# A decoder layer on one Trainium2 core: the filler stream of the first phase yields at every fourth channel tile instead of every second

## The chip, the core and the metric

The kernel runs on one core of a Trainium2 chip. A core has five engines that matter here, each with its own queue of instructions in fixed order: PE (TensorE, matmuls), DVE (VectorE), ACT (ScalarE), POOL (GpSimd) and SP (SyncE, which issues the DMAs). PE writes to PSUM, the others move results from there. The metric is the time of one execution on the device in microseconds.

## What is computed

One hybrid layer on a sequence of 2048 rows of 1024 channels: a norm, one input projection into 26 column tiles of 128, an RWKV-7 group (8 heads, a recurrence with a matrix state), a gated linear attention group (4 heads), an output projection with residual, a norm, a SwiGLU FFN with residual, and a last norm. Cut to what matters:

```python
n = rms_norm(h, rms1_g)
z = n @ w_in                                   # 26 tiles of 128 columns
y_rwkv = rwkv7_mixer(z[..., :D_RWKV_IN], ...)  # S = S*w + (S a) b + v k ; y = S r, step by step
y_gla = gla_mixer(z[..., D_RWKV_IN:], ...)     # in chunks of 64
h = h + concat([y_rwkv, y_gla]) @ w_out
n = rms_norm(h, rms2_g)
h = h + (silu(n @ ffn_gate) * (n @ ffn_up)) @ ffn_down
return rms_norm(h, final_g)
```

## The kernel before

The first phase takes the rows in four blocks of 512. For each block, 26 column tiles `zd` of the input projection are computed. A tile is 8 channel tiles (k = 0 to 7) with three matmuls each: weights and rows are split into a high and a low part, and high x high, high x low and low x high are summed in one PSUM tile (lines 630 to 632). A block so has 26 x 24 = 624 of these matmuls, the phase 2496. Two PSUM tiles, `zd0` and `zd1`, take turns.

All else in the phase are streams, written as Python generators that emit instructions and then `yield`. The list (line 433) has, among others:

- "b" (`stage_b`): the RWKV recurrence, 16 head pairs of 8 steps, four head pairs to a block. A step is `yp` on PE (L1333), `uv` on DVE (L1338), `ch` on PE (L1343), the new state `S` on DVE (L1349), and then `yp` of the next step. After the last step come a norm, the transposes `ytp` (L1380), `gp` (L1383), and the mark `b` with the number of the head pair.
- "a" and "a2": what the recurrence needs for each head pair (`u`, `ssp`, `rbp`, `vp`, `scp`, `bkp`, `bp`; and `atp`, `upp`, `zt`, `xt`, `wtp`, with a long chain `lt`, `lm` on POOL).
- "g" (`gmix`): the linear attention (`gkp`, `gds`, `gsc`, `gop`, `gotp`).
- "e" (`evac`): takes each `zd` tile out of PSUM, in the order of the tiles. It marks `ze` with the tile's number, for which the filler waits two tiles later. In `lora_g`, the evacuation of tile 11 (of tile 14 in the last block), it also waits for a head pair:

```python
        yield used
        if b:
            yield f"b{b * HP - 1}"
```

- "w" (weights: high part on ACT, L605, low part on POOL, L607), "x" and "p" (the normed rows of the next block, transposed by `tch`, L572).
- after the last `zd` tile, the out-projection `op` (32 jobs of 24 matmuls, L902 to L904), whose results are added to `hx`, and the preparation of the FFN's input ("np", "nt"): loads `hk`, transposes `tcn` (L1028), splits into `n` (L1058, L1060). It starts when the last head pair is marked.
- "z", the filler: `zmm`, which issues the `zd` matmuls, and then `out_mm` with those of `op`. It is the only stream marked as filler.

A planner (`Order.run`) puts all streams into one order, by its own estimates of when each engine is free. After each `yield` it picks the stream with the earliest time; the filler's time is at least that at which PE is free, less `AHEAD` (400 ns):

```python
            s = min(q, key=lambda s: (max(s[0], pe - self.AHEAD) if s[4] else s[0], s[1]))
```

So what the filler emits between two yields stands in PE's queue in one piece, and only then can another stream's matmuls follow. A stream that waits for a mark that is not yet set is out of the choice until it is. The FFN behind the phase (`up` with L1573 to L1575, `down`) is put in order by other means, and a few of its matmuls are moved ahead of the last `op`.

Of the kernel before, what the change touches and what calls it, by code (L numbers as in the profile page):

```python
# [269 lines left out]
class K:  # L270
# [341 lines left out]
    def zmm(self, nb):  # L612

        nc = self.nc
        self.zps = {}
        for b in range(nb):
            for i in range(NZ):
                yield f"w{b}.{i}"
                if i > 1:
                    yield f"ze{b}.{i - 2}"  # L620
                else:
                    yield f"prep{b}.{KT - 1 if i else KT // 2 - 2}"
                whi, wlo = self.wz.pop((b, i))
                ps = self.zd("zd", [128, BLK], i)
                for k in range(KT):
                    if not i and not k % 2:
                        yield f"prep{b}.{k}"
                        yield f"prep{b}.{k + 1}"
                    nh, nl = [t[:, k % 2] for t in self.nhl[b, k - k % 2]]
                    nc.tensor.matmul(out=ps, lhsT=whi[:, k, :], rhs=nh, start=(k == 0), stop=False)  # L630
                    nc.tensor.matmul(out=ps, lhsT=whi[:, k, :], rhs=nl, start=False, stop=False)  # L631
                    nc.tensor.matmul(out=ps, lhsT=wlo[:, k, :], rhs=nh, start=False, stop=(k == KT - 1))  # L632
                    if i == NZ - 1 and k % 2:
                        yield ("set", f"zk{b}.{k // 2}")
                    elif k % 2:
                        yield
                self.zps[b, i] = ps
                yield ("set", f"zm{b}.{i}")
# [1125 lines left out]
```

## Time and profile before

| | |
|---|---|
| median of 2 runs | 2765.57 us (2763.24 to 2767.9) |
| the profiled execution | 2761.73 us |
| its span | 2759.9 us, so 1.8 us lie around it |
| mean granted clock of PE | 0.978 |
| busy: PE, DVE, ACT, POOL | 95%, 56%, 44%, 45% of the span |

The span is that of the instructions in the trace. Busy time of PE counts pipelined matmuls as a union, so that a gap in it is a true gap. The granted clock is the share of full TensorE speed that the chip gave; idle time of an engine is put down to what it waited for last.

### The profile page before, as it was taken

Reading aid. Unit: us, or ns where it says so; the run is one execution under the profiler, and the core shown is the slowest. Engines: PE = TensorE matmul, PEld = TensorE weight load, DVE = VectorE, ACT = ScalarE, POOL = GpSimd, SP = SyncE. Lnnn points to the kernel's source line nnn. Section 1 sums busy time; section 2 is a strip of 40 time slices with the busy share of each in tenths; the row PEclk is TensorE's granted clock in tenths of the full one; section 3 lists DMA queues with packets and bytes.
Section 4 is the critical chain, followed back from the end, with each engine's and each line's share of the span. In section 5 each row is a group of like instructions: output and inputs, shape, how many; then the busy total and the mean of one; then the engine's idle time right before and its main releaser. Section 6 shows DMA issues by size and latency. Waiting matters only on the chain.

```text
span 2759.9 us, 40039 instructions
## 1 busy us (share of the span) xinstructions
PE 2616.7 (95%) x14328; PEld 2102.5 (76%) x14328; DVE 1534.0 (56%) x2950; ACT 1219.0 (44%) x2363; POOL 1244.8 (45%) x1866
## 2 busy tenths in 40 slices
PE   6899899989998999999899999999999999999998
PEld 4777677867786777777678787888777888888886
DVE  5456756676666566756655445453647444443354
ACT  7455644665455555544543333342433333332232
POOL 3656555646564476510466566500007555550000
PEclk9999999999998999999999999999999999999999
DMA  4212311232122212456523333265633222224462
GB/s 146 63 58 77 92 55 47 81 100 62 50 69 62 62 59 65 150 176 206 168 92 116 121 118 127 88 214 145 223 127 121 83 84 77 85 85 136 142 225 91
DMA packets 175847, 300.02 MB, mean 109 GB/s; under 512 B 15776, under 2 KB 65664, under 8 KB 175648
## 3 DMA queue, kind: packets, MB, share of 16 engines
q1 hardware_dynamic: 175648, 297.46, 33.8%
q8 instruction: 113, 1.85, 0.3%
q14 instruction: 86, 0.70, 0.1%
HBM read 241.83 MB, written 55.57 MB: 108 GB/s over the span
## 4 chain that ended last, share of the span: by engine, by line
PE 71%; DVE 10%; POOL 6%; DMA 4%; ACT 4%; issue 3%; SPq 1%; DVEq 0%; POOLq 0%; ACTq 0%
PE up L1575 10%; PE up L1574 10%; PE up L1573 10%; PE dn L1648 6%; PE dn L1647 5%; PE dn L1646 5%; PE zd L630 4%; PE zd L632 4%; PE zd L631 4%; DMA hx<-in_x 2%; POOL lm L1249 2%; POOL w_lo L607 2%; POOL lt L1247 2%; PE ch L1343 1%; PE scp L1172 1%
## 5 line engine op out<-in xcount | busy, mean ns | idle before, releaser
L607 POOL TENSOR_TENSOR w_lo<-w_raw,w_hi 128x512 fp32r<-128x512 f32 x208 | 278.9, 1344 | 239.3 <-ACT w_hi L605 203.9
L1070 POOL TENSOR_TENSOR ws<-S,ws 128x512 fp32r<-128x512 f32 x176 | 248.8, 1416 | 289.7 <-ACT ws L1068 280.3
L1579 DVE TENSOR_TENSOR C<-up,C 128x512 f32<-128x512 f32 x308 | 208.4, 689 | 286.5 <-PE up L1575 286.2
L630 PE MATMUL zd<-nh,w_hi 128*128 128x512 f32 x832 | 356.8, 429 | 6.3 <-DVE k L673 3.3
L632 PE MATMUL zd<-nh,w_lo 128*128 128x512 f32 x832 | 333.6, 401 | 8.4 <-POOL w_lo L607 8.4
L631 PE MATMUL zd<-nl,w_hi 128*128 128x512 f32 x832 | 331.1, 398 | 1.5 <-DVE nl L577 1.5
L1574 PE MATMUL up<-n,ws 128*128 128x512 f32 x704 | 278.2, 395 | 4.5 <-DVE n L1060 4.4
L1573 PE MATMUL up<-n,ws 128*128 128x512 f32 x704 | 278.1, 395 | 2.8 <-ACT n L1058 2.8
L1648 PE MATMUL dn<-wd,hh 128*128 128x512 f32 x704 | 279.3, 397 | 0.1
L1575 PE MATMUL up<-n,ws 128*128 128x512 f32 x704 | 278.3, 396 | 0.0
L1647 PE MATMUL dn<-wd,hh 128*128 128x512 f32 x704 | 277.9, 395 | 0.0
L1646 PE MATMUL dn<-wd,hh 128*128 128x512 f32 x704 | 277.4, 394 | 0.0
L1068 ACT CAST ws<-S 128x512 fp32r<-128x512 f32 x176 | 108.5, 620 | 306.7 <-PE up L1575 298.7
L1687 POOL TENSOR_TENSOR h<-h,hx 128x512 f32<-128x512 f32 x12 | 17.8, 1487 | 414.7 <-DMA hx<-hs 311.7
L1249 POOL TENSOR_TENSOR lm<-lm,lt 128x60 f32<-128x60 f32 (+24 forms) x496 | 180.2, 363 | 38.9
L632 PEld LDWEIGHTS zd<-nh,w_lo 128*128 128x128 f32 x832 | 159.4, 192 | 49.4 <-POOL w_lo L607 12.9
L1247 POOL TENSOR_TENSOR lt<-lm,ln 128x60 f32<-128x60 f32 (+24 forms) x496 | 154.3, 311 | 92.9 <-DVE ln L1231 69.3
L1639 DVE TENSOR_TENSOR hh<-hr,hh 128x512 fp32r<-128x512 f32 x88 | 66.2, 752 | 233.7 <-ACT hh L1637 232.9
L630 PEld LDWEIGHTS zd<-nh,w_hi 128*128 128x128 f32 x832 | 160.4, 193 | 38.1 <-issue 4.4
L631 PEld LDWEIGHTS zd<-nl,w_hi 128*128 128x128 f32 x832 | 160.6, 193 | 28.2 <-DVE nl L577 2.3
L1637 ACT CAST hh<-hr 128x512 fp32r<-128x512 f32 x88 | 54.5, 619 | 288.5 <-PE dn L1647 284.0
L1574 PEld LDWEIGHTS up<-n,ws 128*128 128x128 f32 x704 | 133.4, 189 | 36.9 <-DVE n L1060 5.8
(275 smaller groups left out, 5888.5 us busy)
## 6 DMA issues: line engine op xcount, KB each, us to landing
w_raw<-in_win SPq DMA_DIRECT2D x208, 256.0 KB, 2.6
raw<-in_wd SPq DMA_DIRECT2D x88, 512.0 KB, 3.6
raw<-in_wg SPq DMA_DIRECT2D x44, 512.0 KB, 3.5
raw<-in_wu SPq DMA_DIRECT2D x44, 512.0 KB, 3.6
hid<-C SPq DMA_DIRECT2D x88, 256.0 KB, 2.0
hr<-hid SPq DMA_DIRECT2D x88, 256.0 KB, 2.7
mraw<-mix SPq DMA_DIRECT2D x64, 256.0 KB, 4.0
xk<-in_x SPq DMA_DIRECT2D x32, 256.0 KB, 3.7
```

The lines of the kernel that those rows point to most:

```text
L607: nc.gpsimd.tensor_tensor(out=wlo[:, ks, :], in0=raw, in1=whi[:, ks, :].bitcast(F32), op=ALU.subtract)
L630: nc.tensor.matmul(out=ps, lhsT=whi[:, k, :], rhs=nh, start=(k == 0), stop=False)
L631: nc.tensor.matmul(out=ps, lhsT=whi[:, k, :], rhs=nl, start=False, stop=False)
L632: nc.tensor.matmul(out=ps, lhsT=wlo[:, k, :], rhs=nh, start=False, stop=(k == KT - 1))
L1070: eng.tensor_tensor(out=hl[:, 1], in0=src, in1=hl[:, 0].bitcast(F32), op=ALU.subtract)
L1249: nc.gpsimd.tensor_tensor(out=lm[:, 0:j, i0:], in0=lm[:, 0:j, i0:], in1=lt[:, 0:j, i0:], op=ALU.add)
L1573: nc.tensor.matmul(out=ps, lhsT=w[:, 0, ks], rhs=h, start=(k == 0), stop=False)
L1574: nc.tensor.matmul(out=ps, lhsT=w[:, 0, ks], rhs=l, start=False, stop=False)
L1575: nc.tensor.matmul(out=ps, lhsT=w[:, 1, ks], rhs=h, start=False, stop=(k == KT // 2 - 1))
L1646: nc.tensor.matmul(out=ps, lhsT=hh[:, ts], rhs=wh[:, ds], start=(f == 0), stop=False)
L1647: nc.tensor.matmul(out=ps, lhsT=hh[:, ts], rhs=wl[:, ds], start=False, stop=False)
L1648: nc.tensor.matmul(out=ps, lhsT=hl[:, ts], rhs=wh[:, ds], start=False, stop=(f == NF - 1))
```

## The change

In `zmm` the filler yields after every second channel tile, that is, after 6 matmuls. Now it yields after every fourth, after 12. The last tile of a block, which yields after every second channel tile to mark that rows can be overwritten, stays as it is, and so does the first tile of a block, which asks for the prepared rows before each pair. `out_mm` is not touched.

```diff
                     if i == NZ - 1 and k % 2:
                         yield ("set", f"zk{b}.{k // 2}")
-                    elif k % 2:
+                    elif k % 4 == 3:
                         yield
```

Since the planner chooses anew after each yield, the order of nearly all streams shifts with it. Two places show how.

PE before, second block, tile 14: the last filler matmul of 960 and what follows it. (L1343 `ch` of the head pair's last step stands 18 filler matmuls earlier.)

```order
L632 MATMUL zd_4335<-nh_2878,w_lo_4292 128x512
L1284 MATMUL zt_4355<-ui_4315,W_4317 32x32 x16
L1483 MATMUL gotp_4453<-ident_93,gon_4400 128x128 x4
L1298 MATMUL xt_4458<-R_3840,tu_117 64x2x64 x8
L1150 MATMUL vp_4472<-cst_98,v_4009 128x128 x4
```

PE now, the same place, from the second `ch` after the last filler matmul of 960:

```order
L1343 MATMUL ch_4304<-uv_2915,br_2955 128x64 x2
L1333 MATMUL yp_4303<-S3_1_134,ar_2906 128x128
L1343 MATMUL ch_4304<-uv_2915,br_2955 128x64 x2
L1333 MATMUL yp_4303<-S3_0_133,ar_2906 128x128
L1483 MATMUL gotp_4404<-ident_93,gon_4376 128x128 x4
L1272 MATMUL zt_4409<-W_4394,e_3864 32x32 x16
L1343 MATMUL ch_4304<-uv_2915,br_2955 128x64 x2
L1284 MATMUL zt_4409<-ui_4392,W_4394 32x32 x16
L1333 MATMUL yp_4303<-S3_1_134,ar_2906 128x128
L1298 MATMUL xt_4458<-R_3970,tu_117 64x2x64 x8
L1343 MATMUL ch_4304<-uv_2915,br_2955 128x64 x2
```

Steps of the recurrence that stood between runs of filler now follow each other behind the filler. Both orders then go on with the same groups (`wtp`, `vp`, `scp`, `ytp` and so on) to the same next filler matmul.

PE before, the end of the out-projection, with the last `tcn` ahead of it:

```order
L1028 MATMUL tcn<-ident,hk 128x128 x4
L902 MATMUL op<-wo,mh 128x512
L903 MATMUL op<-wo,mh 128x512
L904 MATMUL op<-wo,ml 128x512
L1573 MATMUL up<-n_14029,wg 128x512
L1574 MATMUL up<-n_14030,wg 128x512
L1575 MATMUL up<-n_14029,wg 128x512
L1573 MATMUL up<-n_14222,wg 128x512
```

PE now, the end of the out-projection:

```order
L902 MATMUL op<-wo,mh 128x512
L903 MATMUL op<-wo,mh 128x512
L904 MATMUL op<-wo,ml 128x512
L1574 MATMUL up<-n_13827,wg 128x512
L1575 MATMUL up<-n_13826,wg 128x512
L1573 MATMUL up<-n_14149,wg 128x512
L1028 MATMUL tcn<-ident,hk 128x128
```

Before, 12 groups of `tcn` stand ahead of the last `op` and 24 `up` matmuls between it and the next `tcn`; now it is 9 groups and 3 matmuls.

## Rows read from the trace of the kernel before

**Rows 1.** Windows by stage: length, busy us of each engine, PEclk, DMA, GB/s

```profile
28.00:1116.00 1088.00, 1014.46 (x7129) 813.59 (x7130) 676.93 (x1625) 601.16 (x1245) 642.79 (x1369) 0.96 0.23 71
...
1360.00:1400.00 40.00, 29.55 (x115) 21.54 (x114) 31.09 (x40) 21.54 (x43) 23.88 (x17) 0.87 0.28 90
```

**Rows 2.** One window of 5 us, at a block boundary

```profile
580.00:585.00 5.00, 3.11 (x12) 2.50 (x13) 3.21 (x8) 1.02 (x2) 2.84 (x7) 0.50 0.00 0
```

**Rows 3.** Waits of PE, 28 to 1116: us in total, times, longest

```profile
PE ch L1343 <- DVE uv L1338: 20.9, 12, 4.6
```

**Rows 4.** Six windows around the longest stretches of PE without filler

```profile
396.50:448.60 52.10, 45.51 (x366) 36.29 (x367) 32.35 (x85) 23.41 (x52) 24.45 (x49) 0.89 0.18 52
681.80:724.00 42.20, 38.59 (x331) 30.12 (x329) 30.08 (x83) 24.22 (x53) 19.67 (x35) 1.00 0.19 57
1046.90:1084.30 37.40, 36.86 (x286) 29.80 (x285) 23.22 (x61) 25.11 (x49) 20.36 (x32) 1.00 0.22 64
262.00:300.00 38.00, 35.77 (x290) 26.29 (x289) 28.43 (x74) 21.97 (x49) 7.47 (x15) 0.87 0.28 83
554.00:590.00 36.00, 28.40 (x234) 22.25 (x233) 26.37 (x73) 21.56 (x51) 15.06 (x41) 0.91 0.25 73
832.00:890.00 58.00, 46.33 (x328) 35.78 (x328) 36.94 (x100) 29.59 (x63) 24.67 (x64) 0.82 0.18 54
```

**Rows 5.** Timeline of PE, third block, tile 14: start, us, instruction, idle before

```profile
701.16 0.66 PE L1343 MATMUL ch<-uv,br 128*128 128x64 f32 x4
...
719.99 0.39 PE L1333 MATMUL yp<-S,ar 128*128 128x128 f32 x2
...
721.58 0.66 PE L1343 MATMUL ch<-uv,br 128*128 128x64 f32 x4 [1.21 <-DVE uv L1338]
...
722.91 0.49 PE L1333 MATMUL yp<-S,ar 128*128 128x128 f32 x2 [0.67 <-DVE S L1349]
...
723.96 0.50 PE L630 MATMUL zd<-nh,w_hi 128*128 128x512 f32 x1 [0.56 <-DVE gso L807]
```

**Rows 6.** Timeline of PE, filler and one other group

```profile
601.50 0.40 PE L632 MATMUL zd<-nh,w_lo 128*128 128x512 f32 x1
601.83 1.15 PE L1256 MATMUL upp<-uv,e 128*64 128x64 f32 x32
602.91 0.50 PE L630 MATMUL zd<-nh,w_hi 128*128 128x512 f32 x1
603.25 0.39 PE L631 MATMUL zd<-nl,w_hi 128*128 128x512 f32 x1
...
606.91 0.40 PE L632 MATMUL zd<-nh,w_lo 128*128 128x512 f32 x1
```

**Rows 7.** Timeline of PE, second block, tile 14

```profile
422.25 0.66 PE L1343 MATMUL ch<-uv,br 128*128 128x64 f32 x4
...
442.45 0.39 PE L1333 MATMUL yp<-S,ar 128*128 128x128 f32 x2
...
444.93 0.66 PE L1343 MATMUL ch<-uv,br 128*128 128x64 f32 x4 [2.09 <-DVE uv L1338]
...
446.33 0.80 PE L1333 MATMUL yp<-S,ar 128*128 128x128 f32 x2 [0.74 <-DVE S L1349]
...
448.62 0.77 PE L630 MATMUL zd<-nh,w_hi 128*128 128x512 f32 x1
```

**Rows 8.** Timeline of PE, the last head pair's end

```profile
1247.45 0.55 PE L1343 MATMUL ch<-uv,br 128*128 128x64 f32 x4
...
1258.14 0.60 PE L1380 MATMUL ytp<-ident,y 128*128 128x128 f32 x4
```

**Rows 9.** Timeline of PE, the first FFN matmuls

```profile
1365.65 0.50 PE L1573 MATMUL up<-n,ws 128*128 128x512 f32 x1 [2.76 <-ACT n L1058]
...
1370.26 0.80 PE L1574 MATMUL up<-n,ws 128*128 128x512 f32 x1 [3.41 <-DVE n L1060]
```

## The prediction

> **What bounds the kernel now.** I read the table of stages first. The first phase runs from about 28 to 1116 us; in it PE is busy 1014.46 of 1088 us, while DVE, ACT and POOL are busy 677, 601 and 643 [rows 1]. So PE is the engine that sets the pace, and what the phase loses is 73.5 us in which PE stands idle, plus time at a reduced clock: the mean granted clock is 0.96, and 0.04 x 1088 = 43.5 us. One window shows the reduced level by itself, 0.50, which is 1.2 GHz of 2.4; PE is busy in 3.1 of its 5 us [rows 2]. Together 117 us are lost.
>
> Next the list of waits: the largest wait of PE in this phase is `ch` for `uv`, 20.9 us in 12 cases [rows 3]. That is the recurrence of stream "b": `yp` on PE, `uv` on DVE, `ch` on PE, `S` on DVE, and `yp` again. I set the program's order beside the trace and counted what stands between `yp` and its `ch`. Of 111 such pairs before the last filler matmul, 17 have no filler between them; the waits of `ch` lie almost wholly on those.
>
> Then six windows around the longest stretches without filler, three at tile 14 or 17 and three at block boundaries [rows 4]. Window length less PE busy gives idle time of 6.6, 3.6, 0.5, 2.2, 7.6 and 11.7 us (32.2), and length x (1 - clock) gives 5.7, 0, 0, 4.9, 3.2 and 10.4 us (24.2). So 56 of the 117 us lie in these windows. The first two end at tile 14 of the second and third block, after 960 and 1584 filler matmuls; the last three are the block boundaries. What releases the filler at tile 14 is seen in the third block: `zd` waits for DVE `gso` [rows 5]. The evacuation of tile 12 (`gso`) stands behind `lora_g` in stream "e", and `lora_g` waits for the last head pair of stream "b" of the block before. So the filler can't pass this point before the recurrence has got there, however fast it ran until then. In the fourth block the same dependence sits at tile 17 (2280 matmuls), and there the trace shows next to no loss (0.5 us).
>
> **What the change does to the order.** The matmuls are the same; only their places differ. Runs of filler before the last filler matmul fall from 277 to 198: 178 runs of 6 become 24, and 84 runs of 12 become 162. One run now lasts 12 x 0.229 = 2.75 us instead of 1.4 (0.229 is the pitch of the 17 filler matmuls from 603.25 to 606.91 [rows 6]). The other streams are served half as often, and when it is their turn they go several steps at once. The `yp`-`ch` pairs with no filler between rise from 17 of 111 to 37 of 106, and `ch`-`yp` from 11 to 27; over all streams, steps that depend on the stream's own previous step with no filler between double from 71 to 143. Two thirds of the 143 (96) sit in six long stretches without filler, which lie at 642, 1266 and 1890 filler matmuls (block boundaries), at 960 and 1584, and at 2280. When 888 filler matmuls are out, stream "b" stands four steps further back than before: the filler runs ahead, meets the barrier, and there the recurrence finishes alone.
>
> **The sum, term by term** (against the profiled execution of 2761.7 us).
>
> (a) Tile 14, second block. The stretch without filler holds five `ch` up to the head pair's last, so four steps of the recurrence. A bare step costs 1.59 + 1.33 = 2.9 us from 719.99 to 722.91 [rows 5], or 2.48 + 1.40 = 3.9 us from 442.45 to 446.33 [rows 7]. Four steps and the `gop` group in one of them make 13 to 17 us. From the last `ch` to the release it took 448.62 - 422.25 = 26.4 us with 18 filler matmuls inside [rows 7], and 723.96 - 701.16 = 22.8 us with 24 inside [rows 5]; without filler (4.1 and 5.5 us) 17 to 22. The stretch so takes 30 to 39 us. Most of its groups stand in the first window of the trace, where 52.1 us less 12.3 lost and 72 x 0.229 = 16.5 of filler leave 23 us of work; the second window gives 42.2 - 3.6 - 16.5 = 22 [rows 4]. So 7 to 17 us are idle, 12 in the middle; I add 4 us for the clock, less than the 5.7 of the first window, since slow matmuls partly lie under the chain's waits. About 16 lost, against 12.3 before: **+4** (-2 to +12).
>
> (b) Tile 14, third block: the rows of the order are those of (a), so again 16 lost, against 3.6: **+12** (+5 to +20).
>
> (c) Tile 17, fourth block: one step instead of four, 3 to 4 us, then 17 to 22 to the release, for some 12 us of work by the order; 8 to 14 idle, and 3 for the clock: 14 against 0.5: **+13** (+7 to +19).
>
> (d) Block boundaries lost 7.1, 10.8 and 22.1 us, 40 in all. The new stretches are alike in all three blocks. From the last `ch` to `ytp` the undisturbed chain takes 1258.14 - 1247.45 = 10.7 us [rows 8]; eight other groups lie under it in the order, as much as six of the size of `upp` (1.08 us from 601.83 to 602.91 [rows 6]), 6.5 us. That leaves 4 us idle, and with as much again for the clock as these windows show for each idle microsecond (18.5 to 21.5) and for the wait that follows, 10 each: 30. **-10** (-25 to +5).
>
> (e) Everything else loses 117 - 57 = 60 us. The no-filler pairs there rise from 21 to 43, but pairs with filler between have twice the cover. Bounds: 22 x 1.2 us (20.9 us over 17 pairs) = +26, and -15 if the longer runs swallow a quarter of the 60; I take **+3**, since most new pairs have other streams' work between them.
>
> (f) Fewer changes between filler and other work, 79. The trace shows a pitch of 0.33 from the last filler to `upp` and 0.34 from the first filler after it to the second, instead of 0.229 [rows 6]: 0.2 us for both ends, at most -16 us. But a `ch` or `yp` that is put behind another stream's small matmuls instead of filler pays such an entry as well; **-4**.
>
> (g) After the last filler matmul the out-projection fills PE. Five more steps of the recurrence and a few groups stand there, which the first phase no longer has: the work only moves, **0**.
>
> (h) Start of the FFN. The preparation of its input waits for the last head pair, which now ends at out-projection job 20 instead of 17. So 9 transposed groups `tcn` instead of 12 stand ahead of the last `op`, and before the next `tcn` 3 `up` matmuls instead of 24. In the stage from 1360 to 1400 PE was idle 10.4 us with a clock of 0.87 [rows 1]; two of its waits, each for one missing piece of the input, are 2.76 and 3.41 us [rows 9]. Three more pieces at 3.1 each: **+10** (0 if the wait stays on the last pieces alone, 20 if each costs twice).
>
> The sum is 4 + 12 + 13 - 10 + 3 - 4 + 0 + 10 = +28: 2761.7 + 28 = 2790, and with the 4 us by which the median of the runs lies above the profiled execution, **2793 us**, about 1% slower.
>
> **Rivals.**
> *Faster: the longer runs pay.* If the chain's waits are covered by the other streams' work in the long stretches, (a) to (c) give 0, (d) the full -25, and (f) -16; with +6 for the FFN start the time is 2766 - 35 = 2731. Against it stands that 26 of the 50 no-filler steps that the long stretches gain are the recurrence itself, which nothing shortens. It decides by the idle time at tile 14: under 4 us there it holds. The Trainium skill (TensorEngine Tiling (Array Packing), Key Properties) says that a change of tiling mode drains TensorE; by that rule each of the 79 alternations saved would be worth the full entry price, and (f) would be -16. The trace agrees that an alternation has a price, but shows it at the `upp` group, which uses part of the array's columns, and in the new order such groups meet full-array matmuls of other streams just as well. I give this rival 0.12.
> *Much slower: stretches that do not end with the chain.* If every one of the 72 extra no-filler steps costs the 1.2 us of a waiting `ch`, and the clock adds its share (24.2 to 32.2, so 0.75 for each), that is 72 x 1.2 x 1.75 = 150 us at the outside; half of it makes 2840. It decides by the clock: the six windows would have to show 0.7 or less for 20 us and more. 0.13.
> *No effect: the losses only gather.* At 642, 960, 1266 and 1584 filler matmuls both programs are in nearly the same state; if the recurrence takes as long to get there either way, the long stretches hold what was lost in small pieces before. Then (a) to (e) sum to 0, and (f) and (h) leave 2766 + 6 = 2772. 0.25.
>
> **How the numbers follow.** My own case, 2780 to 2815, has 0.50. The range is 2755 to 2835: it takes in the no-effect case and the bounds of (a) to (h), whose errors are largely independent, and leaves out most of the faster rival and the upper part of the much slower one. Within 2% (55 us), which is what a measurement of this kernel can tell from no change, lies 2711 to 2821; faster by over 2% is 0.01, slower by over 2% 0.13, and 0.86 is left.
>
> **What would show it.** In the new profile: three filler-free stretches of 25 us and more that end at a `zd` released by `gso`, with 8 to 17 us idle in each; waits of `ch` for `uv` and of `yp` for `S` up from 20.9 us to 35 or more; the phase's mean clock at or under 0.96; the last filler matmul 10 to 25 us later, and idle time after the last `op` up by 5 to 15 us. The forecast is wrong if PE stays dense through those stretches, since the recurrence is then not what they wait for, or if the clock stays down after them, since each then costs far more than its idle time.

## The result, and the profile after

The changed kernel takes 2839.51 us (2839.23 to 2839.79, 2 runs) against 2765.57: a ratio of 1.0263, 95% interval 1.0234 to 1.0292. It is 74 us slower, where I had forecast 28. The profiled execution has a span of 2837.5 us (2759.9 before) and a mean granted clock of 0.962 (0.978).

The first view is the table of stages of the changed kernel, cut where the next filler matmul starts after 642, 960, 1266, 1584, 1890 and 2280 of them, at the last one (2496), at the end of the last `op`, and 51 us later. A stretch without filler that begins at one of these counts so lies ahead of the cut. Columns as in [rows 1].

```profile
28.00:296.50 268.50, 243.55 (x1646) 195.68 (x1645) 153.76 (x342) 144.74 (x297) 146.34 (x297) 0.96 0.24 74
296.50:464.20 167.70, 146.71 (x972) 119.18 (x970) 96.98 (x239) 88.56 (x187) 91.84 (x194) 0.88 0.22 67
464.20:606.80 142.60, 129.99 (x939) 106.90 (x938) 86.84 (x212) 70.13 (x148) 76.44 (x168) 0.95 0.21 63
606.80:773.10 166.30, 145.02 (x971) 118.05 (x970) 97.91 (x242) 89.36 (x189) 91.82 (x193) 0.88 0.22 67
773.10:917.40 144.30, 131.65 (x939) 108.17 (x939) 86.96 (x212) 71.28 (x150) 76.58 (x169) 0.93 0.20 62
917.40:1088.60 171.20, 157.78 (x1043) 127.74 (x1042) 98.60 (x233) 86.25 (x173) 99.38 (x205) 0.92 0.19 60
1088.60:1167.40 78.80, 78.75 (x554) 64.37 (x554) 46.50 (x114) 41.27 (x82) 51.59 (x118) 0.99 0.19 58
1167.40:1426.50 259.10, 241.09 (x1360) 191.82 (x1359) 168.09 (x365) 122.89 (x281) 74.10 (x123) 0.95 0.52 171
1426.50:1478.00 51.50, 38.83 (x148) 26.86 (x147) 40.04 (x47) 29.62 (x61) 29.87 (x21) 0.87 0.34 109
```

The same cuts of both kernels, worked out from such rows (idle is length less PE busy; clock loss is length x (1 - clock), which overstates, since idle time at the lower clock stands in both columns):

| up to filler matmul | length before, after | difference | idle before, after | clock loss before, after |
|---|---|---|---|---|
| 642 | 264.3, 268.5 | +4.2 | 17.6, 24.9 | 13.2, 10.7 |
| 960 | 156.3, 167.7 | +11.4 | 15.6, 21.0 | 9.4, 20.1 |
| 1266 | 137.9, 142.6 | +4.7 | 7.3, 12.6 | 5.5, 7.1 |
| 1584 | 137.5, 166.3 | +28.8 | 8.4, 21.3 | 1.4, 20.0 |
| 1890 | 154.7, 144.3 | -10.4 | 14.1, 12.7 | 6.2, 10.1 |
| 2280 | 159.0, 171.2 | +12.2 | 7.5, 13.4 | 3.2, 13.7 |
| 2496 (last) | 78.0, 78.8 | +0.8 | 2.9, 0.1 | 0.0, 0.8 |
| out-projection | 243.9, 259.1 | +15.2 | 12.7, 18.0 | 4.9, 13.0 |
| from there to the end | 1400.3, 1411.0 | +10.7 | | |

So 52 us were lost in the first phase, 15 in the out-projection, 11 behind it. The three segments with the barriers (960, 1584, 2280) hold 52 by themselves, and the others of the phase sum to nothing. Counted without overlap, from the records of PE and of the clock in the two traces, the 77.5 us from 28 us to the end are 42 us more idle time and 41 us for PE busy at the lower clock (half of that time), less 6 us of other changes in PE's work. The windows from the last filler matmul ahead of each barrier to the next one, in the changed kernel:

```profile
411.10:464.20 53.10, 37.52 (x276) 29.63 (x274) 29.88 (x87) 19.14 (x44) 17.70 (x48) 0.66 0.06 20
721.00:773.10 52.10, 36.46 (x275) 28.80 (x274) 29.78 (x87) 19.30 (x44) 17.47 (x47) 0.67 0.06 20
1063.10:1088.60 25.50, 18.78 (x151) 15.31 (x151) 15.72 (x47) 14.68 (x31) 8.18 (x17) 0.76 0.09 31
```

No filler runs for 53, 52 and 25.5 us; PE idles 15.6, 15.6 and 6.7 of them, and the clock loses 18, 17 and 6. The first of the three in pieces of 5 us:

```profile
410.00:415.00 5.00, 2.61 (x16) 2.02 (x14) 4.71 (x12) 1.32 (x4) 4.25 (x10) 1.00 0.15 52
415.00:420.00 5.00, 2.48 (x10) 2.28 (x10) 2.71 (x6) 2.14 (x7) 4.69 (x8) 0.74 0.16 54
420.00:425.00 5.00, 5.00 (x47) 3.56 (x46) 0.57 (x2) 0.59 (x1) 3.83 (x16) 0.50 0.17 54
425.00:430.00 5.00, 4.26 (x18) 2.82 (x18) 1.23 (x3) 1.00 (x2) 0.89 (x4) 0.50 0.00 0
430.00:435.00 5.00, 1.28 (x5) 0.93 (x4) 4.38 (x18) 0.00 (x0) 0.00 (x0) 0.50 0.00 0
435.00:440.00 5.00, 4.82 (x75) 4.24 (x76) 2.03 (x8) 1.48 (x4) 0.00 (x0) 0.50 0.01 3
440.00:445.00 5.00, 4.72 (x36) 3.98 (x38) 0.86 (x3) 1.68 (x6) 0.95 (x3) 0.53 0.00 0
445.00:450.00 5.00, 2.84 (x29) 2.29 (x27) 4.15 (x14) 3.84 (x10) 0.06 (x1) 1.00 0.00 0
```

The clock falls to its lower level (1.2 GHz) in the second window and stays there for some 27 us (2.6 + 20 + 4.7 by the six windows from 415 to 445), while PE is busy 5.00, 4.26, 4.82 and 4.72 of 5 us in four of the windows. The timeline of PE, which answers to [rows 7], tells what stands in them:

```profile
410.89 0.40 PE L632 MATMUL zd<-nh,w_lo 128*128 128x512 f32 x1
...
412.13 0.66 PE L1343 MATMUL ch<-uv,br 128*128 128x64 f32 x4 [0.18 <-DVE uv L1338]
417.52 2.04 PE L1454 MATMUL gsc<-gq,gkk 64*128 64x128 f32 x8 [4.73 <-DVE SG L1442]
...
422.85 0.69 PE L1464 MATMUL gop<-gss,gq 64*64 64x128 f32 x4
...
433.31 1.11 PE L1343 MATMUL ch<-uv,br 128*128 128x64 f32 x4 [3.15 <-DVE uv L1338]
...
442.77 1.11 PE L1343 MATMUL ch<-uv,br 128*128 128x64 f32 x4
...
454.72 1.11 PE L1380 MATMUL ytp<-ident,y 128*128 128x128 f32 x4
...
464.19 0.77 PE L630 MATMUL zd<-nh,w_hi 128*128 128x512 f32 x1
```

A wait of 4.73 us opens the stretch; behind it `gop` takes 0.69 us for what takes 0.44 at full clock, and `ch` 1.11 for 0.66. From the first `ch` of the stretch to the head pair's last it takes 442.77 - 412.13 = 30.6 us, from there to the filler 21.4. `ytp` marks the end of the recurrence; then come `gp`, `gso` and the filler. DVE's `gso` in the three blocks, each just ahead of the filler matmul that ends the window:

```profile
463.28 0.69 DVE L807 SCALAR_TENSOR_TENSOR gso<-gso,zd 128x512 f32<-128x512 f32 x1
...
772.29 0.69 DVE L807 SCALAR_TENSOR_TENSOR gso<-gso,zd 128x512 f32<-128x512 f32 x1
...
1087.62 0.69 DVE L807 SCALAR_TENSOR_TENSOR gso<-gso,zd 128x512 f32<-128x512 f32 x1
```

Of the 15.6 us that PE idles in the first window, `ch` and `yp` of the recurrence wait 6.7; the other 8.9 are groups of other streams, `gsc` with 4.7 and `scp` with 2.9 above all (in the third block 7.0 and 8.6). The waits of PE in the phase (28 to 1167), against [rows 3]:

```profile
PE xt L1298 <- ACT R L1301: 11.9, 4, 3.9
PE tch L572 <- DVE gso L807: 11.6, 3, 3.9
PE ch L1343 <- DVE uv L1338: 11.4, 8, 3.2
PE gsc L1454 <- DVE SG L1442: 10.3, 3, 4.7
PE yp L1333 <- DVE S L1349: 10.1, 12, 1.8
```

`ch` for `uv` fell from 20.9 to 11.4 us; with `yp` for `S` (2.2 before) the recurrence has 21.5 us, where I wanted 35. Other streams in the same stretches wait instead. At the start of the FFN the wait on a missing piece of its input is still there [rows 9]:

```profile
1441.97 0.80 PE L1574 MATMUL up<-n,ws 128*128 128x512 f32 x1 [3.95 <-DVE n L1060]
```

### The profile page after: what moved, and what is told of

It is laid out like the page before. It is cut to its first block, busy times and chain, and to the rows that moved or that the text cites. A ratio compares the mean times of both kernels' runs of the same rounds, so it can differ in the third digit from the quotient of the medians.

```text
span 2837.5 us, 40094 instructions
## 1 busy us (share of the span) xinstructions
PE 2652.4 (93%) x14328; PEld 2139.0 (75%) x14328; DVE 1539.0 (54%) x2950; ACT 1219.0 (43%) x2363; POOL 1252.4 (44%) x1866
## 4 chain that ended last, share of the span: by engine, by line
PE 76%; DVE 11%; POOL 4%; DMA 3%; ACT 3%; issue 2%; SPq 1%; DVEq 0%; POOLq 0%; ACTq 0%
PE up L1575 10%; PE up L1574 10%; PE up L1573 10%; PE dn L1648 5%; PE dn L1647 5%; PE zd L630 5%; PE dn L1646 5%; PE zd L632 5%; PE zd L631 5%; PE ch L1343 1%; POOL lm L1249 1%; DMA hx<-in_x 1%; PE xt L1298 1%; PE scp L1172 1%; POOL lt L1247 1%
## 5 line engine op out<-in xcount | busy, mean ns | idle before, releaser
L607 POOL TENSOR_TENSOR w_lo<-w_raw,w_hi 128x512 fp32r<-128x512 f32 x208 | 272.1, 1316 | 179.0 <-ACT w_hi L605 174.7
L1247 POOL TENSOR_TENSOR lt<-lm,ln 128x60 f32<-128x60 f32 (+24 forms) x496 | 169.7, 342 | 96.8 <-DVE ln L1231 72.7
L1349 DVE SCALAR_TENSOR_TENSOR S<-ch,Pm,st 64x64 f32<-64x64 f32 x256 | 72.2, 282 | 173.3 <-PE ch L1343 140.2
```

Source lines behind the costliest of these rows:

```text
L607: nc.gpsimd.tensor_tensor(out=wlo[:, ks, :], in0=raw, in1=whi[:, ks, :].bitcast(F32), op=ALU.subtract)
```

## The experiments

The theories that the expectations name: **L** (lag), mine: the recurrence falls behind the filler and finishes alone at the barrier; the loss lies there. **P** (price): each step that follows its stream's own with no filler between pays about 1 us wherever it stands (74 us over 143 - 71 = 72 steps). **C** and **W**: in the stalls it is the clock, or the waits, that cost. **B**, formed later: the block boundaries and what stands behind the last filler matmul carry the loss. **T** and **K**: the clock falls because of a wait, or because of the small matmuls. In all runs but e2, e5 and e6 the stream "np" also waits for the mark "wo2.1" before it starts. That changes the order only behind the last filler matmul, and no run has it alone: in e17, whose order up to there is that of the changed kernel but for the added matmuls, the out-projection takes 264.6 us instead of 259.1. Differences of some 5 us behind the last filler matmul are so not told apart from it. Four kernels (e9, e10, e17, e18) add matmuls of which nobody reads the result; none leaves anything out.

**Which blocks** (in place of `k % 4 == 3`):

```diff
-                    elif k % 4 == 3:
+                    elif k % 4 == 3 or b == nb - 1 and k % 2:   # e1: runs of 12 in blocks 0 to 2
+                    elif k % 4 == 3 or b < nb - 1 and k % 2:    # e2: in the last block
```

> Runs of 12 in the first three blocks, runs of 6 in the last (the FFN's preparation also waits for the mark wo2.1, which is early). Theory L (lag and barrier: runs of 12 hold the recurrence back, and at the tile whose evacuation waits for it the filler stands still while the chain finishes alone at a low clock): the stalls at 960 and 1584 filler matmuls stay as in the changed kernel, some 39 us over the first three blocks, the stall at 2280 and the late FFN start go: 2800 to 2810. Theory P (each step with no filler before it costs about 1 us, wherever it stands): 125 such steps against 143 and 71, so three quarters of the 74 us: 2820.

> Runs of 6 in the first three blocks, runs of 12 in the last. Theory L: the recurrence is not behind when the last block begins, so the order shows no long stretch at 2280, but 23 steps of it instead of 17 are left for the out-projection, which with the FFN's start costs the 26 us seen in the changed kernel: 2785 to 2795. Theory P: 78 no-filler steps against 71: 2773.

Measured 2818.94 (ratio 1.0179, interval 1.0154 to 1.0203) and 2783.54 (1.0061, 1.0038 to 1.0085), against 2766.64. The excesses, 52 and 17 us, add up to 69 of the 74: blocks 0 to 2 and the last one count nearly separately. In the second, the segment to 2280 is 15 us shorter than before, the out-projection 13 longer and what follows 18 longer. So for the last block the price is paid behind the last filler matmul, where six more recurrence steps stand than before. P was nearer on the first, L on the second.

**Where the barrier is.** The tile with the barrier was moved from place 11 (14 in the last block) to place 18, with runs of 12 (e3) and of 6 (e4):

```diff
-    SEQZ = [..., ZV + 1, ZVG + 1, ZG, ZOG, ZK + 2, ...]
+    SEQZ = [..., ZV + 1, ZVG + 1, ZK + 2, ZR + 2, ZV + 2, ZOG, ZK + 3, ZR + 3, ZV + 3, ZG, ...]   # SEQL alike
```

> Runs of 12, and the column tile whose evacuation waits for the recurrence moved from place 11 (14 in the last block) to place 18, so that the filler meets the barrier seven tiles later. To be compared with the same tile order with runs of 6. Theory L: the two stretches of 53 us at 960 and 1584 are gone, smaller ones at 1020 to 1032 and 1644 to 1656 (12 us of work in two parts) take their place; 30 to 40 us slower than the same order with runs of 6, not 74. Theory P: 132 no-filler steps against 63: 70 us slower than it.

> Runs of 6 with the same late place of that column tile. Theory L: the barrier is met after the recurrence has passed it, and the 12 us lost at tile 14 of the second block go: 2750 to 2770. Theory P: 63 no-filler steps against 71: 2757. It is the base for the run with runs of 12.

Measured 2822.40 and 2774.92, 47.5 us apart instead of 74; L wanted 30 to 40 and P 70, and the second time lies above both ranges. The windows of the kernel with runs of 12, from 642 to 960 and from 960 to 1266:

```profile
300.10:429.70 129.60, 122.77 (x799) 98.20 (x798) 79.10 (x184) 72.46 (x151) 84.13 (x181) 0.96 0.22 72
429.70:597.50 167.80, 150.90 (x1112) 122.57 (x1111) 105.96 (x268) 87.92 (x187) 86.00 (x179) 0.91 0.22 65
```

With the barrier gone from 960, the stretches of 53 us at 960 and 1584 are gone too: that they belong to the barrier is shown. None takes their place at the new barrier (1104 and 1728 matmuls, where the filler halts for 1.8 us); the longest new ones are 14 us, at 1032 and 1656. The segment to 960 is 38 us shorter than in the changed kernel, 24 of them PE's busy time and 14 idle; the next is 25 us longer, 21 of them busy and 4 idle, so that most of this is work that went along. Of the price a third goes, not more: the other two thirds don't need the 53 us stretches.

**How long the runs are**: `elif True` (runs of 3, e5) and `elif k == KT - 1` (runs of 24, e6).

> Runs of 3: the filler yields after every channel tile. Theory L: the recurrence is served as soon as it is ready, it was hardly behind with runs of 6, so little is to be had: 2750 to 2775. Theory P: 49 no-filler steps against 71, 22 us faster: 2744. A price of the alternations themselves (0.1 to 0.2 us for each of 70 more runs) would give 2773 to 2780.

> Runs of 24: a yield only at a whole column tile. The order holds 36 us of work without filler at 960 and at 1584, and 22 + 14 at 2184 and 2280. Theory L with the low clock in the stalls (53 us for 20.6 of work): 92 us each, so about 70 us more than the changed kernel: 2890 to 2930. Theory P: 248 no-filler steps against 143: 2950.

Measured 2761.01 (0.9972, 0.9958 to 0.9987) and 2964.63 (1.0705, 1.0677 to 1.0733), against 2768.73. Runs of 3, 6, 12 and 24 give 2761, about 2767, 2840 and 2965; runs of 3 are the best version found, 8 us under before, inside L's range (P wanted 2744). The rule of the Trainium skill that the rival "Faster" weighs (TensorEngine Tiling (Array Packing), Key Properties) is that a change of tiling mode drains TensorE. If each of the 71 more alternations of runs of 3 paid the 0.2 us of (f), that would be 14 us; the kernel became faster, so such a price, if it is paid, is outweighed. The kernel before also shows the slower entry behind `ch`, a group on the whole array (0.31 us from 1113.03 to 1113.34 instead of 0.229), so that these rows don't tie it to the tiling mode. Runs of 24 went past both theories: the mean clock is 0.93, a loss of 0.07 x 2962 = 207 us.

**Matmuls added in the stalls.** Four 128x512 matmuls of a constant ahead of each group while the filler waits for a mark, in the changed kernel (e9) and the kernel before (e10):

```diff
+        if stall and name in ("yp", "gsc", "upp", "gotp", "zt", ...):
+            for _ in range(4):
+                nc.tensor.matmul(out=v, lhsT=self.one, rhs=..., start=True, stop=True)   # 128x512, into the group's tile
```

> The changed kernel with four extra matmuls of 128x512 (fp32r, of a constant, into a PSUM tile that the next group overwrites) ahead of eleven kinds of groups, only where the order has the filler waiting for a mark: 64 of them at 960 and at 1584 filler matmuls, 32 at 2280, some 70 at the block boundaries, 0.23 us each, 15 us of PE work in a stall of 53. Theory C (the slow clock makes half of the stall: its matmuls run at 1.2 GHz): the granted clock in the stalls rises from 0.6 to 0.9 and more, they shorten to some 42 us: 2805 to 2825. Theory W (the waits of the chain set the length, the clock doesn't matter): the extra work fills waits at best: 2840 to 2870.

> The kernel before with the same extra matmuls where its order has the filler waiting for a mark, some 120 in all, 28 us of PE work. Theory C: part of the 44 us that the low clock costs in the first phase comes back: 2740 to 2765. Theory W: 2766 to 2795.

Measured 2861.04 and 2772.72, against 2768.73, both in W's ranges. In the changed kernel 280 matmuls (64 us at 0.23) raise the excess from 74 to 92 us; the clock loss to 960 fell from 20.1 to 14.3 and to 1584 from 20.0 to 10.4, but the segments grew to 179 and 173 us. Some time came back, less than was put in. In the kernel before, 124 matmuls (28 us) cost 4 us, and the clock loss, as in the last table of this part, fell by 12. This doesn't separate C from W: the added matmuls wait for the same PSUM tile as the group behind them, and so fill no wait for a tile.

**Which tiles.** Runs of 12 ahead of the barrier (tiles 0 to 13, e7) or behind it (14 to 25, e8):

```diff
+                    elif k % 4 == 3 or i > 13 and k % 2:   # e7
+                    elif k % 4 == 3 or i < 14 and k % 2:   # e8
```

> Runs of 12 in the column tiles 0 to 13 of each block only, runs of 6 behind. In the order the stretch at 960 holds 12.2 us of work with 14 steps without filler between (20.6 and 27 in the changed kernel, 11.6 and 13 before), that at 1584 17.6 us with 21 steps (20.6 and 27; 5.2 and 5 before); 100 such steps in all, 20 recurrence steps behind the last filler matmul. Theory L: what was lost ahead of 960 goes back nearly to before (at most +6), ahead of 1584 about +20 stay, with +8 behind the last filler: 2785 to 2805. Theory P: 29 steps more than before at 1 us, +30 evenly spread: 2796, with the excess ahead of 1584 no more than 10.

> Runs of 12 in the column tiles 14 to 25 of each block only, runs of 6 ahead. In the order the stretch at 960 holds 13.5 us of work with 17 steps without filler between, that at 1584 11.6 with 13, and 24 recurrence steps stand behind the last filler matmul (17 before, 22 in the changed kernel); 95 such steps in all. Theory L: +4 ahead of 960, +8 ahead of 1584, +20 behind the last filler matmul (out-projection and start of the FFN): 2785 to 2805, more than half of the excess behind the last filler matmul. Theory P: 24 steps more at 1 us, 2790, nearly all of it ahead of the last filler matmul.

Measured 2762.91 (0.9993, 0.9982 to 1.0003) and 2826.34 (1.0209, 1.0184 to 1.0235), against 2766.35. Both theories missed both. In e7 the segment to 1584 is 10 us longer than before (L wanted 20, P no more than 10), and those to 1890 and 2280 give 16 back each; the first and the last of these three:

```profile
589.70:737.10 147.40, 133.80 (x945) 107.43 (x944) 96.66 (x230) 84.14 (x179) 80.05 (x163) 0.94 0.24 76
...
876.30:1019.00 142.70, 142.06 (x1010) 115.02 (x1009) 96.33 (x216) 79.57 (x160) 83.68 (x173) 1.00 0.21 68
```

In e8 the excess is spread: +8, +5, +10, +19, -4, -6 and +3 us up to the last filler matmul, segment by segment, and +20 in the out-projection, with hardly more lag at 936 than e7 (28 steps out, 29 in e7). What sets it apart is seen at the second boundary, where `gop` and its neighbours stand in the same row as in the changed kernel. First e8, its windows there, two filler matmuls and one `gop`; the fence after it is the changed kernel's.

```profile
576.00:580.00 4.00, 2.04 (x15) 1.70 (x16) 3.67 (x9) 3.13 (x8) 0.34 (x2) 0.96 0.00 0
580.00:584.00 4.00, 4.00 (x13) 3.39 (x14) 1.23 (x2) 0.00 (x0) 0.00 (x0) 0.50 0.01 4
...
583.25 0.63 PE L630 MATMUL zd<-nh,w_hi 128*128 128x512 f32 x1
583.68 0.63 PE L631 MATMUL zd<-nl,w_hi 128*128 128x512 f32 x1
...
584.00:594.00 10.00, 10.00 (x99) 7.12 (x98) 2.98 (x10) 2.09 (x5) 0.00 (x0) 0.50 0.00 0
...
586.41 0.80 PE L1461 MATMUL gop<-gV,gat 128*128 128x128 f32 x2
```

```profile
578.00:582.00 4.00, 2.00 (x15) 1.60 (x14) 3.77 (x9) 3.25 (x8) 1.37 (x6) 1.00 0.00 0
...
584.00:594.00 10.00, 7.64 (x118) 5.68 (x116) 5.87 (x22) 2.46 (x6) 1.14 (x4) 1.00 0.00 1
...
585.71 0.49 PE L1461 MATMUL gop<-gV,gat 128*128 128x128 f32 x2
```

PE is busy 10.00 of 10.00 us at a clock of 0.50 in one, 7.64 at 1.00 in the other, with more matmuls done. So a stretch of the same work has no fixed price: in e8 the clock fell just ahead of it, behind 4 us in which PE was busy for 2.04. The changed kernel has the same groups there with like waits, PE busy for 2.00 of 4 us, and its clock stayed at 1.00: neither the order nor these waits alone tell whether it falls.

**Who goes first.** The planner's preference turned, with runs of 12 (e11) and of 6 (e12):

```diff
-    AHEAD = 400.0
+    AHEAD = -700
```

> The changed kernel with the planner's preference turned: the filler's time is PE's free time plus 700 ns instead of less 400 ns, so that the other streams go first more often. The runs of filler are the same 12 matmuls (200 runs, 198 in the changed kernel), and the steps that follow their predecessor with no filler between are even more, 165 against 143 (71 before); but the order no longer has a long stretch without filler (the longest holds 8.0 us of work, 20.6 in the changed kernel), since the recurrence no longer lags, and 16 instead of 22 of its steps stand behind the last filler matmul. Theory L (lag and barrier: the loss is what the recurrence still has to do alone where the filler must wait for it): 2765 to 2790, no stretch of 25 us without filler, idle plus clock loss ahead of 960 and of 1584 like before. Theory P (each step without filler between pays, 1 us apiece from 74 us over 72 steps): 2766 + 94 = 2860.

> The kernel before with the same turn of the planner's preference (plus 700 ns instead of less 400). 119 steps without filler between (71 before), longest stretch 10.5 us of work (11.6 before), 14 steps of the recurrence behind the last filler matmul (17 before). Theory L: 2750 to 2780. Theory P: 2766 + 48 = 2814.

Measured 2788.74 (1.0077, 1.006 to 1.0094) and 2813.86 (1.0179, 1.0154 to 1.0204), against 2766.35. With the same runs of 12 and more steps without filler (165), 51 of the 74 us are gone; P wanted 2860 and falls. The segments to 960 and to 1584 of e11 are 33 us shorter than in the changed kernel (those to 642 and 1266 are 16 longer):

```profile
312.10:446.30 134.20, 123.72 (x846) 99.11 (x846) 85.98 (x198) 79.40 (x167) 66.22 (x131) 0.95 0.25 79
605.80:739.90 134.10, 123.58 (x845) 98.92 (x846) 85.88 (x198) 79.39 (x167) 66.19 (x131) 0.95 0.25 79
```

No stretch without filler over 12 us is left in e11 up to the last filler matmul. But with runs of 6 the same turn costs 48 us, against L and as P had it. In the profiled execution, the fastest of four (2806.45 us, clock 0.977), it is idle time, 122 us up to the last `op` instead of 86; the other three had 0.967 to 0.971, so that the clock has a part in the median. Under the turned preference the longer runs are the faster ones, so run length has no price that holds for every order.

**Which stretches carry it.** Runs of 12 in tiles 0 to 19 (e13: barrier stretches as in the changed kernel, boundaries short), 6 to 25 (e14: the reverse), 18 to 25 (e15: no lag), and none, with runs of 3 in 14 to 25 (e16):

```diff
+                    elif k % 4 == 3 or k % 2 and not 0 <= i < 20:    # e13; e14: 6 <= i < 26; e15: 18 <= i < 26
+                    elif (k % 2 if i < 14 else True):                # e16
```

> Runs of 12 in the column tiles 0 to 19 of each block, runs of 6 in 20 to 25. The filler-free stretches at the barriers are those of the changed kernel (20.6, 20.6 and 13.1 us of work at 960, 1584 and 2280; 26 recurrence steps out at 936), those at the block boundaries are short (6.0 us at 642, 1266 and 1890; 12.9 in the changed kernel). Theory L (the barrier stretches carry the loss): 2810 to 2830, with the losses of the changed kernel at 960 and 1584 (40 us idle plus clock in each of the two segments). Theory B (the boundaries and what stands behind the last filler carry it): 2770 to 2790.

> Runs of 12 in the column tiles 6 to 25 of each block, runs of 6 in 0 to 5. The stretches at the block boundaries are those of the changed kernel (12.9 us of work), those at the barriers shorter (12.9, 12.9 and 6.5 us at 960, 1584 and 2280, 20.6, 20.6 and 12.3 in the changed kernel; 11.6 and 5.2 before); 24 recurrence steps stand behind the last filler matmul (22 in the changed kernel, 17 before). Theory L: 2795 to 2815. Theory B: 2820 to 2840, as much as with runs of 12 behind the barrier alone (2826).

> Runs of 12 in the column tiles 18 to 25 of each block only. The recurrence does not lag (32 steps out at 936, 31 before), no stretch at a barrier is over 6.1 us of work; the longest are 14.0 (first boundary) and 10.0 and 9.0 (second). Theory L: 2760 to 2780. Theory B: 2785 to 2805, the loss at the boundaries.

> No run of 12: runs of 6 in the column tiles 0 to 13 of each block as before, runs of 3 in 14 to 25. 52 steps without filler between (71 before, 49 with runs of 3 throughout). Both theories: 2750 to 2765, since runs of 3 throughout gave 2761; B says nearer to 2750, as the tiles behind the barrier are where run length counts; L says 2761 to 2765.

Measured 2814.54 (1.017), 2843.99 (1.0267), 2780.02 (1.0041) and 2772.18 (1.0014, 0.9999 to 1.003), against 2767.84. For e13 L said 2810 to 2830, with 40 us lost in each of two segments; they show 39 and 40:

```profile
284.50:454.60 170.10, 149.61 (x1011) 120.74 (x1009) 101.16 (x265) 91.71 (x195) 92.59 (x194) 0.89 0.21 67
585.90:756.50 170.60, 150.71 (x1010) 121.52 (x1009) 102.84 (x266) 91.24 (x194) 92.38 (x195) 0.88 0.22 68
```

So the barrier stretches with the out-projection's +15 make 47 us without long stretches at the boundaries; the segments that end there (642, 1266, 1890) are even 8, 7 and 23 us shorter than before, so that part of what stands at the barriers is only gathered there. In e14 B's number nearly came (2844 against 2820 to 2840), not its place: the segment to 1584 is still 24 us longer than before, though its stretch holds 12.9 us of work instead of 20.6, the boundaries are +10, +10 and -10, the out-projection +26. The losses are not parts that add up; each order gets its own. e15, without the lag, is at the edge of L's range; e16 is above both.

**The long wait filled.** In the changed kernel, 64 matmuls of a constant ahead of `gsc` in the two stalls (e17), or right behind it (e18); the order of the first phase is otherwise the same in e17, while in e18 some groups of the two stretches change places. The edit, shortened:

```diff
+            for _ in range(64):
+                nc.tensor.matmul(out=ch_part, lhsT=self.one, rhs=self.one, start=True, stop=True)   # 128x128
             for i in range(NPR):
                 nc.tensor.matmul(out=ps[:, i, :], lhsT=k[hq, ts], rhs=q[hq, ts], start=True, stop=True)   # gsc
```

> The changed kernel with 64 matmuls of a constant, 128x128, ahead of the gsc group that opens the two filler-free stretches at 960 and 1584, where PE waits 4.73 us for DVE SG; they go into a part of the PSUM tile ch that nobody reads. All other instructions of the first phase stand in the same order. At some 0.06 us each they are 3.8 us and lie in the wait. Theory T (the clock falls because of the wait): in both stretches it stays near full until the next long wait, 10 us each come back, 2812 to 2828. Theory K (the small matmuls of the stretch bring it down whether PE waits or not): 2836 to 2848, clock 0.5 from about 420 to 440 as in the changed kernel.

> The same 64 matmuls in the same two places, but behind the gsc group, so that the 4.73 us wait ahead of it stays and the matmuls lie on the path. Both theories: the clock falls as in the changed kernel; 64 matmuls at 0.06 to 0.12 us are 4 to 8 us in each of two places, partly under the chain's waits: 2838 to 2855. If the matmuls themselves keep the clock up, whatever stood ahead of them, it would be 2825 to 2838.

Measured 2869.54 and 2870.35, against 2772.33; inconclusive, by a price of mine. The timeline and windows of e17:

```profile
413.36 13.91 PE L1455 MATMUL ch<-one 128*128 128x128 f32 x64 [2.82 <-ACT y L1357]
...
415.00:420.00 5.00, 5.00 (x25) 5.00 (x25) 0.12 (x1) 0.00 (x0) 4.37 (x12) 0.50 0.32 105
...
430.00:435.00 5.00, 5.00 (x55) 3.78 (x56) 0.29 (x2) 0.58 (x1) 0.00 (x0) 0.74 0.01 3
```

The matmuls began after a wait of their own, 2.82 us, and took 0.217 us each (13.91 / 64), not 0.06: three times the wait they were to fill. The clock fell in those 2.82 us and stood at 0.50 past 430, with PE busy all the time since 413.36; it came back between 430 and 435, in the groups behind, with PE still busy. So T and K stay untold, and a PE that the profile calls busy does not bring the clock back soon.

The clock over all kernels: clock loss is span x (1 - mean clock) of an execution, here as the mean over all executions of a kernel, less the mean over those of the kernel before that stand beside it (65 to 68 us; for the change 66.5, the middle of these). Idle time at the lower clock is in it, so it overstates what the clock costs. The excess is by the medians.

| kernel | excess us | clock loss more than before us |
|---|---|---|
| runs of 12 (the change) | 74 | 44 |
| e14, e8, e3 | 76, 60, 56 | 46, 50, 38 |
| e1, e12, e13 | 52, 48, 47 | 42, 16, 43 |
| e11, e2, e15 | 22, 17, 12 | 9, 14, 2 |
| e4, e16, e7, e5 | 8, 4, -3, -8 | 9, 4, 4, -16 |
| e6 | 196 | 136 |
| e18, e17, e9, e10 (matmuls added) | 98, 97, 92, 4 | 59, 64, 21, -12 |

In the change and in e14, e8, e3, e1, e13, e2 and e6 the clock loss is more than half of what the kernel loses; in e11, e12 and e15 it is less, and e12 loses mostly by idle time. The executions of the kernel before differ alike with no change of order at all: of the 19 beside e5 and e6 the fastest took 2761.02 us at a mean clock of 0.978, the slowest 2779.39 at 0.973, 18 us more time with 14 us more clock loss. So time goes with the clock here; how much of it would come back at the full clock is not shown.

## Why the prediction was wrong

**What bounds the kernel, and the mechanism**: right in part. The recurrence lags (26 steps out at 936 filler matmuls instead of 31), the filler meets the barrier, and the stretches I named are there, at 960, 1584 and 2280. DVE's `gso` is done at 463.97, 772.98 and 1088.31, the next `zd` starts 0.2 to 0.3 us later each time. That the long stretches belong to the barrier is shown by e3 and e13; that the lag makes them, by e11 and e15, which have neither. What was wrong is that in them PE waits for the recurrence: over half of the idle time there is other streams' (8.9 of 15.6 us), and the sign that I had named, 35 us of the recurrence's waits, came out at 21.5, against 23.1 before. Nor does the barrier carry the whole price: e3 keeps two thirds of it without the 53 us stretches.

**(a) and (b), the step that failed.** "Four steps and the `gop` group in one of them make 13 to 17 us." They took 30.6 us in both blocks (412.13 to 442.77 and 721.89 to 752.53); the rest of the chain took 21.4 and 20.6, inside my 17 to 22. So the stretches last 53 and 52 us instead of 30 to 39. The term left out the 4.73 us in which `gsc`, a group of another stream in the same queue, waits for DVE SG, and it priced the steps at full clock, while all that stands behind that wait ran at 0.50: "I add 4 us for the clock" stands against 18 and 17 us by the windows, 15 and 14 if only PE's busy time counts. I had taken the 5.7 of [rows 4] as a ceiling, but there fillers followed soon behind each wait. Idle time, 15.6 us in both, lies inside my 7 to 17, but by luck: I had made it of the bare chain less the work, and most of it is other waits. The term (a) came to +11.4, close to my upper bound, (b) to +28.8 against +12 (+5 to +20).

**(c)**: here the chain was right, 3.7 us for its one step and 21.2 to the release. The sum, +12.2 against +13, was right by luck: idle 6.7 instead of 8 to 14 and clock 6 instead of 3 cancel.

**(d), (e), (f)**: the three boundary segments sum to 4.2 + 4.7 - 10.4 = -1.5 against -10 for (d), inside its bounds, (e) and (f) mixed into it.

**(g), the second step that failed**: "the work only moves, 0". The out-projection took 15 us more: 5 are idle, and PE's busy time is 10 longer (231.2 to 241.1). About 4 of these 10 are the work that moved there, 60 matmul records, which the first phase no longer has; the rest ran at the lower clock. With 24 recurrence steps behind the last filler matmul instead of 17 (e8, e14), the same stage takes 264 and 270 us instead of 244. So work that moves is not free where it lands.

**(h)**: +10.7 against +10, right in number, and partly by luck: I had counted waits alone, but idle time behind the last `op` rose by 4.8 us (33.7 to 38.5) and PE's busy time by 5.9. That the missing `tcn` groups make it was not tested alone.

The misses are 7 + 17 - 1 + 9 + 2 (what is left of the phase) + 15 + 1 = 50 us, which is 78 - 28.

**The rivals.** "Much slower" had the price, 2840, and its sign that the clock decides; but its condition, six windows at 0.7 or less for 20 us, held in two, and its mechanism, each step without filler at 1.2 us and more, fell with e11 and e7. "Faster" needed under 4 us idle at tile 14 and had 15.6. "Only gather" is refuted by the segments: the losses at 960 and 1584 are new, only 10 us at 1890 came back.

**What stays open**: what part of a barrier stretch is the clock's and what the chain's, since no experiment set one without the other; where the two thirds of the price that e3 keeps come from, beyond the segments in which they lie; and why runs of 12 behind the barrier (e8, e14) cost so much more than runs ahead of it (e7) at nearly the same lag.

## What to carry to other kernels

When a filler gets coarser, look for marks that it must wait for, and count what the slowest chain has still to do when it gets there; then price all that stands in that stretch, the other streams' groups and their waits too, and price it twice, once as idle time and once as time at half clock. The finest yields tried were best here (3 matmuls a run, by 8 us), and where a planner sets the order, its preference and the run length have to be tuned together: one reversed the sign of the other. A single term set to zero because "the work only moves" wants a row of the stage that it moves to.

## What the runs showed of the hardware

The granted clock did not follow PE's busy share. It stood at 0.50 while PE was busy 10.00 of 10.00 us with small matmuls (e8, 584 to 594) and 5.00 of 5.00 with back-to-back 128x128 ones (e17, 415 to 420), and at 1.00 with PE busy 2.84 of 5 (the changed kernel, 445 to 450). The falls shown here came with waits of PE: one of 4.73 us, one of 2.82, and in e8 several that left it busy 2.04 of 4 us; but in the changed kernel the same groups with like waits (2.00 of 4 us busy from 578 to 582) left the clock at 1.00. In e17 PE was busy without a gap from 413.36 on, and the clock came back only between 430 and 435. The Trainium skill (TensorE: Matmul & The Clock Gate, What's actually happening) says that activity releases the throttle; in e17 the throttle is released in the end, but behind more than 16 us of a PE that the profile calls fully busy, so that its busy share alone does not tell the clock, and here the measurement decides.

A 128x128 matmul of a constant with its own weights took 0.217 us at the lower clock (e17). A 128x512 one takes 0.43 there (e8, 583.25 to 583.68) and 0.229 at full clock [rows 6]. So a quarter of the columns took half the time, and small matmuls are a dear way to fill a wait.
